# Queries and keys of two head groups transposed by VectorE and through DRAM, with 15 slots and 6 split units

## The chip, the cores and the metric

One core of a Trainium2 chip runs the whole program. The metric is the device time of one execution in microseconds (us). Engines are named as in the profile: PE is TensorE (matmul), PEld its weight load, DVE is VectorE, ACT is ScalarE, POOL is GpSimd, SP the engine that issues the DMAs.

## The reference, cut to what matters

Two layers work on x of 256 tokens and 2048 columns, in float32. Each layer mixes tokens and then channels:

```python
h = rmsnorm(x, norm_mix_pre[l])
proj = h @ w_in[l]                                # 2048 -> 5120 columns
a_q, a_k, a_v, b_glu, c_q, c_k, c_v, d_q, d_k, d_v = jnp.split(proj, split_at, axis=-1)
out_a = diff_attention(a_q, a_k, a_v, ...)        # 4 heads, two maps of 64 each, rotary
out_b = conformer_conv(b_glu, ...)                # 31 taps, layernorm, 512x512 product
out_c = gqa_axial_attention(c_q, c_k, c_v, ...)   # 4 query heads, 2 key heads of 128
out_d = neighbourhood_attention(d_q, d_k, d_v, rpb)
mixed = jnp.concatenate([out_a, out_b, out_c, out_d], axis=-1) @ w_out[l]
x = x + rmsnorm(mixed, norm_mix_post[l])
h = rmsnorm(x, norm_ffn_pre[l])
f = (silu(h @ ffn_gate[l]) * (h @ ffn_up[l])) @ ffn_down[l]   # 2048 -> 5632 -> 2048
x = x + rmsnorm(f, norm_ffn_post[l])
```

The scores of A and C are products over the head's columns, so queries and keys are needed with those columns on the partitions: transposed.

## The kernel before, in words

**Products.** Each weight is read once from DRAM in pieces of 128 rows by 1024 columns, two to a load (a `Raw`, 1 MB, three buffers). A piece is a unit. ScalarE rounds it to the short format of TensorE (`whi`, `split_hi`), VectorE computes what the rounding left (`wlo`, `split_lo`), and a product is x's rounded half times both, plus x's residual times `whi`. A step (`products`) is one unit, one of the two blocks of 128 tokens, and two PSUM banks of 512 columns: six matmuls. `NSPLIT` buffers hold split units.

**Order.** The program's order is written out by `run`, step by step. Ahead of a step's products come, in this order, the loads tied to it (`pre`), `tick`, and `splits_to`. `tick` advances every other piece of work (a generator) whose time has come by a planner's clock `at`, which adds a cost to each instruction; `wait` adds 0.2 to that clock where a step's left operand has not been issued yet. Each engine then works its own queue in that order, and semaphores do the rest. `plan` (line 261) cuts a pass over the weights into groups of units: a group's steps run for the first tokens, then for the second, and a unit's buffers come free with the second (`used`). REGULAR groups have four units. FIRST, used for the first pass of the gate/up phases and of layer 1's input phase, is 6, 5, 5. LAST is 4, 4, 3, 5.

`splits_to` (line 242) says how far the splits run ahead. It is called with `used + NSPLIT` and the unit of the step:

```python
        while self.next_split < n:
            r = self.next_split // 2
            self.loads_to(r + 1)
            self.split_hi(self.units[self.next_split])
            if self.next_split > self.next_lo:
                self.lo_next()
            self.next_split += 1
        while self.next_lo < min(needed + 1, n):
            self.lo_next()
```

**Phases of a layer.** Input (five passes, B, C, A, D and V, 160 steps), output (two passes over the mixed columns, in the order C, B, A, D in the first), gate/up (11 passes), down (two passes). Between the end of one phase and the next, `post` normalises x, adds it, and `transpose_x` (line 421) turns it: TensorE transposes four blocks of 128 into PSUM, ScalarE writes the rounded half of `xT`, VectorE the residual half.

**Heads.** When C's projection has left PSUM, `norm_c` (line 837) normalises and rotates it in `rotC`; `rope_a` (line 736) does A's in `rotA`. Then `attn_c` (line 873) and `attn_a` (line 794) call `heads_transposed` (line 762): four (for C's keys two) TensorE transposes into a PSUM bank of the pool `tp`, and a ScalarE copy into `qkC` or `qkA`, for each block of tokens. The heads follow, two at a time: `head_c` claims one of the two `sc` banks for its scores, `head_a` both; maximum on VectorE, exponentials on ScalarE, the probabilities transposed by TensorE (`probs_transposed`). D does the same with one bank (`head_d`). `out_a` (line 999) starts when V has left PSUM and all four A heads are done, and writes `mixA`; the output phase needs it at its 17th step.

**Through DRAM.** The hidden layer of the gate/up phase already goes another way: `ffn_half` (line 531) lets VectorE transpose 32x32 blocks, SP writes them to DRAM (`h_blocks`), and `turned` (line 551) reads them back so that the blocks' order is put right (`ht`), from where ScalarE and VectorE make `hT`.

**Slots.** All wider working tiles share one pool of `SLOTS` buffers of 8 KB per partition. A split unit has two buffers of 4 KB.

Of the kernel before, what the change touches and what calls it, by code (L numbers as in the profile page):

```python
# [11 lines left out]
F32 = mybir.dt.float32  # L12
F32R = mybir.dt.float32r
AF = mybir.ActivationFunctionType
# [5 lines left out]
P = 128  # L20
L = 2
S = 256
T = S // P
# [9 lines left out]
HD = 128  # L33
RPB = 15 * 31

SLOTS = 14
NRAW = 3
NSPLIT = 7
RAMP = 3
CONV_LEAD = 1.5  # L40
LATENCY = 0.4
LC_AT = 12
STATS_AT = 20
# [59 lines left out]
class Trunk:  # L103
# [214 lines left out]
    def tick(self):  # L318

        todo, self.gens = self.gens, []  # L320
        kept = []
        for entry in todo:
            g, ready = entry
            if ready <= self.at["PE"]:
                self.chain = 0.0
                try:
                    next(g)
                except StopIteration:
                    continue
                entry[1] = self.chain + LATENCY if self.chain else 0.0  # L330
            kept.append(entry)
        self.gens = kept + self.gens

# [402 lines left out]
    def rope_a(self, phase, pair, tok):  # L736
# [21 lines left out]
        if tok == T - 1:  # L758
            yield from self.until(T, "a", phase)
            yield from self.attn_a()  # L760

    def heads_transposed(self, dst, src, n):

        nc = self.nc
        for tok in range(T):
            yield from self.claim("tp")
            b = self.bank("tp", (4, P))
            for h in range(n):
                nc.tensor.transpose(b[:, h], src(tok)[:, h * P:(h + 1) * P], self.ident)
            yield  # L770
            nc.scalar.activation(dst[:, 0:n, tok * P:(tok + 1) * P], b[:, 0:n], AF.Copy)
            yield
            self.free("tp")
# [18 lines left out]
        self.free("tp")  # L792

    def attn_a(self):
        qk = self.slot([2, 4, S], F32, "qkA")
        for i in range(2):
            yield from self.heads_transposed(qk[:, i], lambda t: self.rotA[:, t, i], 4)
        self.ptA = self.slot([4, T, S], F32, "ptA")
        work = self.slot([2, 2, T, S], F32, "workA")
        for h in range(4):  # L800
            yield from self.until(h - 1, "done_a", self.l)
            self.spawn(self.head_a(h, qk, work[:, h % 2]))
            yield

    def head_a(self, h, qk, p):
        nc = self.nc
        yield from self.claim("sc", 2)
        banks = [self.bank("sc", (T, S)) for _ in range(2)]
        for t in range(T):
            for m in range(2):  # L810
                rows = slice(m * 64, (m + 1) * 64)
                nc.tensor.matmul(banks[m][:, t], qk[rows, 0, h, t * P:(t + 1) * P], qk[rows, 1, h],
                                 start=True, stop=True)
        yield
        mx, sm = self.small(4, "mx"), self.small(4, "sm")
        for m in range(2):
            nc.vector.reduce_max(mx[:, 2 * m:2 * m + 2], banks[m], axis=AX.X)
        nc.vector.tensor_scalar(mx, mx, -0.125, None, op0=ALU.mult)
        for m in range(2):
            self.exps(p[:, m], banks[m], mx[:, 2 * m:2 * m + 2], sm[:, 2 * m:2 * m + 2], 0.125)  # L820
        yield
        self.free("sc", 2)
        nc.vector.reciprocal(sm, sm)
        nc.vector.tensor_scalar(sm[:, 2:4], sm[:, 2:4], self.neg_lam[:, self.l:self.l + 1], None,
                                op0=ALU.mult)
        for t in range(T):
            nc.scalar.activation(p[:, 1, t], p[:, 1, t], AF.Copy, scale=sm[:, 2 + t:3 + t])
        yield
        for t in range(T):
            nc.vector.scalar_tensor_tensor(p[:, 0, t], p[:, 0, t], sm[:, t:t + 1], p[:, 1, t],  # L830
                                           op0=ALU.mult, op1=ALU.add)
        yield
        yield from self.probs_transposed(p[:, 0], self.ptA[:, h])
        self.mark("done_a", self.l)
# [36 lines left out]
            yield from self.attn_c()  # L871

    def attn_c(self):
        qk = self.slot([6, S], F32, "qkC")
        yield from self.heads_transposed(qk[:, 0:4], lambda t: self.rotC[:, t, 0:512], 4)
        yield from self.heads_transposed(qk[:, 4:6], lambda t: self.rotC[:, t, 512:768], 2)
        self.mixT[2] = self.slot([2, 4, S], F32R, "mixC")
        work = self.slot([2, 2, T, S], F32, "workC")
        for h in range(4):
            yield from self.until(h - 1, "mix_c", self.l)  # L880
            self.spawn(self.head_c(h, qk, work[:, h % 2]))
            yield

    def softmax(self, p, src, scale):
# [20 lines left out]
        yield  # L905
        self.free("tp")

    def head_c(self, h, qk, work):
        nc = self.nc
        yield from self.claim("sc")  # L910
        b = self.bank("sc", (T, S))
        for t in range(T):
            nc.tensor.matmul(b[:, t], qk[:, h, t * P:(t + 1) * P], qk[:, 4 + h // 2], start=True, stop=True)
        yield
        p, pt = work[:, 0], work[:, 1]
        sx = self.softmax(p, b, HD ** -0.5)
# [133 lines left out]
    def build(self):  # L1050
# [4 lines left out]
        for l in range(L):  # L1055
# [9 lines left out]
            if l == 0:  # L1065
                self.steps[n0 + 8].pre += [self.tables]
                self.steps[n0 + 44].pre += [lambda: self.spawn(self.lambdas())]
            self.steps[n0 + 108].pre += [lambda l=l: self.load_bias(l)]
            self.steps[n0 + 120].pre += [self.mask_bias]
            w = a["w_out"][l]  # L1070
            n0 = len(self.steps)
            order = [4 * "ABCD".index(g) + i for g in OUT_ORDER for i in range(4)]
# [94 lines left out]
```

## Time and profile before

| what | value |
|---|---|
| time, median of 3 runs | 2179.38 us (2179.23 to 2179.76) |
| time of the profiled execution | 2179.6 us |
| its span, first to last instruction | 2177.8 us |
| TensorE busy | 2156.9 us, 99% of the span |
| VectorE busy | 1271.1 us, 58% |
| ScalarE busy | 1093.8 us, 50% |
| mean granted TensorE clock | 0.999 |
| bytes moved by DMA | 447.52 MB, 205 GB/s over the span |

A busy share says how long an engine had an instruction in it. TensorE's matmul records overlap, so a share of 99% says that it hardly ever stood empty, and the spacing of the records, not their length, says what one costs. Nearly all instructions carry line 89, the line of the helper that records their cost, so work is found by the names of its tiles.

### The profile page before, as it was taken

How to read it: one execution, taken by the hardware profiler on the slowest of the kernel's cores; microseconds unless marked ns; L12 is line 12 of the kernel's file. 1: busy time of each engine (PE TensorE's matmuls, PEld its weight loads, DVE VectorE, ACT ScalarE, POOL GpSimd, SP SyncE). 2: the span in 40 equal slices, each digit the busy share in tenths (PEclk: the TensorE clock that was granted, in tenths of full speed). 3: DMA queues.
4: the chain of work that ended last, by engine and by line, in shares of the span. 5: the costliest groups of instructions: out<-in, count | busy, mean ns of one | idle time of the engine just before them, and what ended most of it. 6: DMA issues, size and time to landing. Idle time of an engine off the chain costs nothing.

```text
span 2177.8 us, 25210 instructions
## 1 busy us (share of the span) xinstructions
PE 2156.9 (99%) x9720; PEld 1781.5 (82%) x9720; DVE 1271.1 (58%) x1520; ACT 1093.8 (50%) x1398; POOL 28.6 (1%) x38
## 2 busy tenths in 40 slices
PE   8999999999999999999999999999999999999998
PEld 7888887888888888888878888878888888888886
DVE  5898555555555554444468975555555555554444
ACT  6656754544444444343465576554444444443432
POOL 0000000000000000000000000000000000000000
PEclk9999999999999999999999999999999999999999
DMA  7556446766676666555575563557667666765553
GB/s 277 194 177 184 170 149 221 232 213 212 223 222 213 212 223 221 214 193 194 211 237 182 191 188 136 210 187 241 213 221 223 213 213 222 223 213 213 193 218 130
DMA packets 200281, 447.52 MB, mean 205 GB/s; under 512 B 20704, under 2 KB 43744, under 8 KB 197856
## 3 DMA queue, kind: packets, MB, share of 16 engines
q1 hardware_dynamic: 200016, 445.87, 60.5%
q8 instruction: 76, 1.25, 0.2%
q14 instruction: 45, 0.37, 0.1%
q10 hardware_dynamic: 144, 0.03, 0.0%
HBM read 425.93 MB, written 19.92 MB: 205 GB/s over the span
## 4 chain that ended last, share of the span: by engine, by line
PE 97%; ACT 1%; DVE 1%; issue 0%; DMA 0%; DVEq 0%; POOLq 0%; ACTq 0%
PE acc L89 93%; PE tp L89 3%; PE sc L89 1%; ACT whi L89 0%; DVE xT L89 0%; ACT workA L89 0%; DVE x L89 0%; ACT L89 0%; DMA x<-in_x_dram 0%; ACT xT L89 0%; DVE mx L89 0%; DVE wlo L89 0%; ACT conv L89 0%; ACT qkD L89 0%; ACT junk L89 0%
## 5 line engine op out<-in xcount | busy, mean ns | idle before, releaser
L89 PE MATMUL acc<-whi,xT 128*128 128x512 f32 x4096 | 1293.3, 393 | 6.8 <-DVE xT L89 2.9
L89 PEld LDWEIGHTS acc<-whi,xT 128*128 128x128 f32 x4096 | 769.9, 188 | 171.5 <-DVE xT L89 5.5
L89 PE MATMUL acc<-wlo,xT 128*128 128x512 f32 x2048 | 799.1, 390 | 0.5 <-DVE wlo L89 0.5
L89 ACT ACTIVATE whi<-raw,gains 128x1024 fp32r<-128x1024 f32 x512 | 582.6, 1150 | 388.6 <-PE acc L89 365.8
L89 DVE SCALAR_TENSOR_TENSOR wlo<-raw,gains,whi 128x1024 fp32r<-128x1024 f32 x512 | 641.8, 1278 | 216.9 <-ACT whi L89 208.8
L89 PEld LDWEIGHTS acc<-wlo,xT 128*128 128x128 f32 x2048 | 385.3, 188 | 78.6 <-DVE wlo L89 1.0
L89 DVE TENSOR_TENSOR wlo<-raw,whi 128x1024 fp32r<-128x1024 f32 x240 | 292.5, 1223 | 260.6 <-ACT whi L89 243.9
L89 PE MATMUL acc<-whi,hT 128*128 128x512 f32 x1408 | 434.1, 389 | 0.0
L89 ACT ACTIVATE whi<-raw 128x1024 fp32r<-128x1024 f32 x240 | 253.7, 1060 | 304.3 <-PE acc L89 304.1
L89 PEld LDWEIGHTS acc<-whi,hT 128*128 128x128 f32 x1408 | 264.3, 188 | 54.9
L89 PE MATMUL acc<-wlo,hT 128*128 128x512 f32 x704 | 273.9, 389 | 0.0
L89 PEld LDWEIGHTS acc<-wlo,hT 128*128 128x128 f32 x704 | 132.1, 188 | 27.3
L89 DVE TENSOR_TENSOR hT<-ht,hT 128x1024 fp32r<-128x1024 f32 x22 | 27.0, 1225 | 142.3 <-ACT hT L89 142.3
L89 DVE SCALAR_TENSOR_TENSOR h<-acc,rstd,h 128x512 f32<-128x512 f32 x44 | 33.0, 751 | 120.9 <-ACT h L89 120.9
L89 DVE SCALAR_TENSOR_TENSOR conv<-uT,lc,conv 128x256 f32<-128x256 f32 x240 | 99.3, 480 | 0.0
L89 ACT ACTIVATE hT<-ht 128x1024 fp32r<-128x1024 f32 x22 | 23.3, 1059 | 107.5 <-DMA ht<-h_blocks 107.5
L89 ACT ACTIVATE h<-acc,rstd 128x512 f32<-128x512 f32 x44 | 30.3, 688 | 81.5 <-PE acc L89 81.2
L89 ACT ACTIVATE junk<-acc 128x512 bf16<-128x512 f32 x32 | 19.1, 595 | 55.9 <-PE acc L89 53.0
L89 PE MATMUL acc<-whi,mixC 128*128 128x512 f32 x128 | 44.7, 402 | 0.0
L89 PE MATMUL acc<-whi,mixB 128*128 128x512 f32 x128 | 42.2, 397 | 0.0
L89 DVE TENSOR_TENSOR mg<-acc,gpost 128x512 f32<-128x512 f32 x32 | 21.3, 686 | 35.8 <-PE acc L89 19.5
L89 PE MATMUL acc<-whi,mixD 128*128 128x512 f32 x128 | 41.6, 391 | 0.0
(136 smaller groups left out, 962.2 us busy)
## 6 DMA issues: line engine op xcount, KB each, us to landing
raw<-in_ffn_gate_dram SPq DMA_DIRECT2D x176, 512.0 KB, 3.9
raw<-in_ffn_up_dram SPq DMA_DIRECT2D x176, 512.0 KB, 5.1
raw<-in_ffn_down_dram SPq DMA_DIRECT2D x88, 1024.0 KB, 5.0
raw<-in_w_in_dram SPq DMA_DIRECT2D x63, 1024.0 KB, 5.1
raw<-in_w_out_dram SPq DMA_DIRECT2D x32, 1024.0 KB, 5.0
raw<-in_w_in_dram SPq DMA_DIRECT2D x34, 512.0 KB, 4.7
h_blocks<-blocks SPq DMA_DIRECT2D x44, 256.0 KB, 5.5
ht<-h_blocks SPq DMA_DIRECT2D x88, 128.0 KB, 5.3
```

The source lines that it names most:

```text
L89: return f(*args, **kw)
```

## The change

VectorE transposes queries and keys of A and C in blocks of 32x32 (`crossed`). SP writes the blocks to DRAM, one DMA per block of tokens, and reads them back with four DMAs of 32 partitions each. ScalarE copies the queries into order, for A into the buffer that later takes the probabilities, for C back into `rotC`; the keys are used where they landed, in runs of 32 columns. The planner lets 9.0 pass by its clock after each of the two transfers. The pool has one slot more and the splits one unit less. The bias loads of D and their mask are tied to later steps.

```diff
--- before.py
+++ after.py
@@ -33,11 +33,12 @@
 HD = 128
 RPB = 15 * 31
 
-SLOTS = 14
+SLOTS = 15
 NRAW = 3
-NSPLIT = 7
+NSPLIT = 6
 RAMP = 3
 CONV_LEAD = 1.5
+TRANSFER = 9.0
 LATENCY = 0.4
 LC_AT = 12
 STATS_AT = 20
@@ -324,10 +325,12 @@
             if ready <= self.at["PE"]:
                 self.chain = 0.0
                 try:
-                    next(g)
+                    transfer = next(g)
                 except StopIteration:
                     continue
                 entry[1] = self.chain + LATENCY if self.chain else 0.0
+                if transfer:
+                    entry[1] = max(entry[1], self.at["PE"] + TRANSFER)
             kept.append(entry)
         self.gens = kept + self.gens
 
@@ -759,6 +762,32 @@
             yield from self.until(T, "a", phase)
             yield from self.attn_a()
 
+    def crossed(self, srcs, n, name, dst):
+
+        w = n * P
+        hd = self.pd.tile([S, w], F32, name=self.name(name))
+        qk = self.slot([2048], F32, name)
+        for tok in range(T):
+            bt = qk[:, tok * 1024:tok * 1024 + w]
+            for h0 in range(0, n, 4):
+                m = min(4, n - h0)
+                out = bt.rearrange("p (q k n) -> p k q n", q=4, k=n)[:, h0:h0 + m]
+                src = srcs(tok, h0, m).rearrange("p (k q n) -> p k q n", k=m, q=4)
+                self.nc.vector.transpose(out, src)
+            yield
+            self.nc.sync.dma_start(hd[tok * P:(tok + 1) * P, :], bt)
+        yield True
+        qk = qk[:, 0:8 * n * 32].rearrange("p (t k n) -> p t k n", t=8, k=n)
+        for q in range(4):
+            src = hd[:, q * n * 32:(q + 1) * n * 32].rearrange("(t p) m -> p t m", p=32)
+            self.nc.sync.dma_start(qk[32 * q:32 * q + 32].rearrange("p t k n -> p t (k n)"), src)
+        yield True
+        for h, (out, m) in enumerate(dst):
+            q = qk[:, :, h * m:(h + 1) * m].rearrange("p t h n -> p h t n")
+            self.nc.scalar.activation(out.rearrange("p h (t n) -> p h t n", t=8), q, AF.Copy)
+        yield
+        return qk
+
     def heads_transposed(self, dst, src, n):
 
         nc = self.nc
@@ -792,24 +821,23 @@
         self.free("tp")
 
     def attn_a(self):
-        qk = self.slot([2, 4, S], F32, "qkA")
-        for i in range(2):
-            yield from self.heads_transposed(qk[:, i], lambda t: self.rotA[:, t, i], 4)
         self.ptA = self.slot([4, T, S], F32, "ptA")
+        q = self.ptA[:, :, 0]
+        qk = yield from self.crossed(lambda t, h, n: self.rotA[:, t, h // 4], 8, "qkA", [(q, 4)])
         work = self.slot([2, 2, T, S], F32, "workA")
         for h in range(4):
             yield from self.until(h - 1, "done_a", self.l)
-            self.spawn(self.head_a(h, qk, work[:, h % 2]))
-            yield
-
-    def head_a(self, h, qk, p):
+            self.spawn(self.head_a(h, q[:, h], qk[:, :, 4 + h], work[:, h % 2]))
+            yield
+
+    def head_a(self, h, q, k, p):
         nc = self.nc
         yield from self.claim("sc", 2)
         banks = [self.bank("sc", (T, S)) for _ in range(2)]
         for t in range(T):
             for m in range(2):
                 rows = slice(m * 64, (m + 1) * 64)
-                nc.tensor.matmul(banks[m][:, t], qk[rows, 0, h, t * P:(t + 1) * P], qk[rows, 1, h],
+                nc.tensor.matmul(banks[m][:, t], q[rows, t * P:(t + 1) * P], k[rows],
                                  start=True, stop=True)
         yield
         mx, sm = self.small(4, "mx"), self.small(4, "sm")
@@ -871,14 +899,13 @@
             yield from self.attn_c()
 
     def attn_c(self):
-        qk = self.slot([6, S], F32, "qkC")
-        yield from self.heads_transposed(qk[:, 0:4], lambda t: self.rotC[:, t, 0:512], 4)
-        yield from self.heads_transposed(qk[:, 4:6], lambda t: self.rotC[:, t, 512:768], 2)
+        q = [self.rotC[:, t, 0:512].rearrange("p (h s) -> p h s", h=2) for t in range(T)]
+        qk = yield from self.crossed(lambda t, h, n: self.rotC[:, t, h * P:(h + n) * P], 6, "qkC", [(x, 2) for x in q])
         self.mixT[2] = self.slot([2, 4, S], F32R, "mixC")
         work = self.slot([2, 2, T, S], F32, "workC")
         for h in range(4):
             yield from self.until(h - 1, "mix_c", self.l)
-            self.spawn(self.head_c(h, qk, work[:, h % 2]))
+            self.spawn(self.head_c(h, q[h // 2][:, h % 2], qk[:, :, 4 + h // 2], work[:, h % 2]))
             yield
 
     def softmax(self, p, src, scale):
@@ -905,12 +932,12 @@
         yield
         self.free("tp")
 
-    def head_c(self, h, qk, work):
+    def head_c(self, h, q, k, work):
         nc = self.nc
         yield from self.claim("sc")
         b = self.bank("sc", (T, S))
         for t in range(T):
-            nc.tensor.matmul(b[:, t], qk[:, h, t * P:(t + 1) * P], qk[:, 4 + h // 2], start=True, stop=True)
+            nc.tensor.matmul(b[:, t], q[:, t * P:(t + 1) * P], k, start=True, stop=True)
         yield
         p, pt = work[:, 0], work[:, 1]
         sx = self.softmax(p, b, HD ** -0.5)
@@ -1065,8 +1092,8 @@
             if l == 0:
                 self.steps[n0 + 8].pre += [self.tables]
                 self.steps[n0 + 44].pre += [lambda: self.spawn(self.lambdas())]
-            self.steps[n0 + 108].pre += [lambda l=l: self.load_bias(l)]
-            self.steps[n0 + 120].pre += [self.mask_bias]
+            self.steps[n0 + 120].pre += [lambda l=l: self.load_bias(l)]
+            self.steps[n0 + 130].pre += [self.mask_bias]
             w = a["w_out"][l]
             n0 = len(self.steps)
             order = [4 * "ABCD".index(g) + i for g in OUT_ORDER for i in range(4)]
```

## Rows read from the trace of the kernel before

**Rows 1.** The page: busy time of each engine; the chain that ended last, by engine.
```profile
PE 2156.9 (99%) x9720; PEld 1781.5 (82%) x9720; DVE 1271.1 (58%) x1520; ACT 1093.8 (50%) x1398; POOL 28.6 (1%) x38
...
PE 97%; ACT 1%; DVE 1%; issue 0%; DMA 0%; DVEq 0%; POOLq 0%; ACTq 0%
```

**Rows 2.** TensorE's waits: who waited for whom, us in total, times, longest.
```profile
PE acc L89 <- DVE wlo L89: 0.5, 1, 0.5
```

**Rows 3.** The chain in order of time: start us, us, what; the longest piece of layer 0.
```profile
384.33 701.14 PE acc L89 x3093
```

**Rows 4.** Timeline of TensorE around a group of two and one of four transposes.
```profile
144.65 0.38 PE L89 MATMUL tp<-ident,rotC 128*128 128x128 f32 x2
...
145.10 0.40 PE L89 MATMUL acc<-wlo,xT 128*128 128x512 f32 x1
...
177.57 0.60 PE L89 MATMUL tp<-ident,rotA 128*128 128x128 f32 x4
...
178.24 0.39 PE L89 MATMUL acc<-wlo,xT 128*128 128x512 f32 x1
```

**Rows 5.** Groups by form: busy us, mean ns of one, idle us before.
```profile
L89 ACT ACTIVATE whi<-raw 128x1024 fp32r<-128x1024 f32 x240 | 253.7, 1060 | 304.3 <-PE acc L89 304.1
...
L89 DVE STREAM_TRANSPOSE blocks<-h 128x512 f32<-128x512 f32 x44 | 31.0, 705 | 0.0
...
L89 ACT ACTIVATE hT<-ht 128x1024 fp32r<-128x1024 f32 x22 | 23.3, 1059 | 107.5 <-DMA ht<-h_blocks 107.5
...
L89 PE MATMUL sc<-qkA 64*128 64x256 f32 x64 | 9.1, 402 | 0.0
...
L89 PE MATMUL tp<-ident,rotA 128*128 128x128 f32 x32 | 4.8, 272 | 0.0
```

**Rows 6.** DMA issues: operation, count, KB each, median us from issue to landing.
```profile
h_blocks<-blocks SPq DMA_DIRECT2D x44, 256.0 KB, 5.5
ht<-h_blocks SPq DMA_DIRECT2D x88, 128.0 KB, 5.3
...
x<-x_spill SPq DMA_DIRECT2D x6, 1024.0 KB, 8.7
```

**Rows 7.** Timeline of TensorE at the start of layer 0's gate/up phase.
```profile
372.78 0.60 PE L89 MATMUL tp<-ident,x 128*128 128x128 f32 x4
...
373.45 0.40 PE L89 MATMUL acc<-wlo,xT 128*128 128x512 f32 x1
...
374.61 1.03 PE L89 MATMUL tp<-ident,x 128*128 128x128 f32 x8
376.38 0.50 PE L89 MATMUL acc<-whi,xT 128*128 128x512 f32 x1 [0.74 <-ACT xT L89]
```

**Rows 8.** Timeline of VectorE in the same stretch.
```profile
370.04 1.27 DVE L89 SCALAR_TENSOR_TENSOR wlo<-raw,gains,whi 128x1024 fp32r<-128x1024 f32 x1
...
374.05 0.69 DVE L89 TENSOR_TENSOR xT<-tp,xT 128x512 fp32r<-128x512 f32 x1 [0.81 <-ACT xT L89]
```

**Rows 9.** Timeline of TensorE in layer 0: C begins, A ends, A's output products begin.
```profile
135.26 0.60 PE L89 MATMUL tp<-ident,rotC 128*128 128x128 f32 x4
...
149.00 1.02 PE L89 MATMUL sc<-qkC 128*128 128x256 f32 x4
...
245.32 0.74 PE L89 MATMUL tp<-ident,workA 128*128 128x128 f32 x4 [0.19 <-DVE workA L89]
...
265.64 1.95 PE L89 MATMUL sc<-vAD,ptA 128*128 128x128 f32 x16
```

**Rows 10.** Timelines of VectorE and TensorE: mixA's last write and first use, both layers.
```profile
292.87 0.69 DVE L89 TENSOR_TENSOR mixA<-tp,mixA 128x512 fp32r<-128x512 f32 x1 [2.13 <-ACT mixA L89]
...
298.10 0.39 PE L89 MATMUL acc<-whi,mixA 128*128 128x512 f32 x1
...
1376.01 0.69 DVE L89 TENSOR_TENSOR mixA<-tp,mixA 128x512 fp32r<-128x512 f32 x1
...
1379.29 0.39 PE L89 MATMUL acc<-whi,mixA 128*128 128x512 f32 x1
```

## The prediction

> **What bounds the kernel now.** I read the page first, engine shares and the chain that ended last [rows 1]: TensorE is busy 99% of the span and holds 97% of the chain. Then TensorE's own waits [rows 2]: on the residual half of a split weight (`wlo`) it waited once, 0.5 us in all, so today no split is late. Then the chain in order of time [rows 3]: 3093 products of 512 columns follow one another in 701.14 us, 0.227 us each. A step is six of them, 1.37 us. So the time changes in two ways only: work leaves or joins TensorE's queue, or TensorE begins to wait. Anything under 0.2% (4.4 us) a measurement of this kernel cannot tell from no change.
>
> **What leaves TensorE.** Per layer, 16 transposes for A (four groups of four) and 12 for C (two groups of four, two of two): 56 in two layers. Their price is read from the queue around them. From the start of a group of four to the second product after it is 0.67 us (177.57 to 178.24), less one product 0.23: 0.44. For a group of two 0.45 less 0.23: 0.22 [rows 4]. So 12 x 0.44 + 4 x 0.22 = **6.2 us off**. The record of one transpose is 272 ns long [rows 5], but records overlap; 0.11 us each is what the queue loses. The Trainium skill, "TensorE: Matmul & The Clock Gate", Part 4: PE-mode transpose, gives about 275 ns for one in a kernel's context; the trace agrees on the record's length (272), not on its price here, and by 0.275 the 56 would be worth 15.4 us instead of 6.2.
>
> **What joins the other engines, at no cost while TensorE leads.** VectorE gets per layer four 512-wide transposes for A, two of 512 and two of 256 for C: 8 at most at 705 ns [rows 5], 5.6 us, and VectorE is 58% busy [rows 1]. ScalarE loses eight PSUM copies per layer and gets one copy of 1024 elements for A, two of 512 for C, from data cut in runs of 32; `hT`'s copy, cut the same way, takes 1059 ns for 1024, a plain one 1060 [rows 5]. So a little less work than before. SP gets 12 more DMAs per layer (two writes and four reads for each of A and C). A write waits on SP for its transposes, and weight loads stand behind it; that is short, because the order issues it a step later. The write of 256 KB takes 5.5 us, a read of 128 KB 5.3; here they are twice that or less (512 and 256 KB for A). Even 1024 KB from DRAM takes 8.7 [rows 6]. The order allows 9.0 by its own clock, in which a step costs 1.29 against 1.37 traced: about 9.6 us. So ScalarE's copies, and the weight splits queued behind them, should not wait. From above: each of the four read-backs late by 2 us, most of it inside the margin of the splits; I take 0.
>
> The score products now read the keys in runs of 32 columns at a stride. No row shows TensorE doing that. From below nothing; from above the price doubles, for A 9.1 us of records [rows 5], and about as much again for C. ScalarE reads the same runs without surcharge [rows 5], so I take 0; the upper end gets a chance of 0.02 and stays outside the range. The bias loads and the mask, moved 12 and 10 steps later, still precede D's scores; cost 0.
>
> **Six split units instead of seven.** In steady groups of four a split is issued five steps before its use instead of six, 6.9 us instead of 8.2, for 1.06 + 1.27 us of work [rows 5, 8]. No stall. But the first group of a phase has six units (FIRST: the gate/up phase of both layers, the input phase of layer 1; three places). `splits_to` issues a residual only with the *next* unit's rounded half, or when its step needs it. With seven buffers unit 6 may be split during unit 0's step, and that issues unit 5's residual. With six buffers unit 6 must wait for a buffer, so unit 5's residual is issued right ahead of its own products, after the tick of that step. That tick holds the transposes of x's third block: behind them stands, on VectorE, the residual of that block.
>
> Layer 0's gate/up start shows the price. Now VectorE finishes unit 5's residual at 371.31 (370.04 + 1.27), and TensorE reads it at 373.45. After: transposes of x at 372.78, ScalarE's rounding, VectorE's xT 374.05 to 374.74 [rows 7, 8] (that pair begins when the transposes end, so it does not come earlier), then the residual, 1.27 more, about 375.95. TensorE reads it at 376.0 instead of 373.45: **2.55 us**. Does it come back? The next eight transposes (374.61) and the product that waits for them (376.38) [rows 7] lie behind unit 5's products in TensorE's queue, so they move with it. The pattern repeats in all three places: **+7.6 us**. Bounds: 0, if the order puts the tick elsewhere, and 4 each (12), if the second group's splits, one step later too, also come late.
>
> **C and A come later.** C's first transposes are at 135.26 and its first scores at 149.00, 13.7 us [rows 9]. After: two transfers of 9.6 and about four steps of 1.4, 25 us. So C's heads move by some eight or nine steps, and A's heads, which queue for the same two score banks, with them. A step here takes 1.75 us with its insertions (149.00 to 245.32 is 55 steps), so A's last probabilities (245.32) come near 261 in layer 0; with their copy the output products, now at 265.64 [rows 9] for lack of V, would start about 5.4 us later, in layer 1 about 3.2 by the same count (two steps). The margins now: mixA's last write ends at 293.56 for a use at 298.10 (4.5 us); in layer 1 1376.70 for 1379.29 (2.6) [rows 10]. Short by 0.9 and 0.6: **+1.5 us**. Bounds 0 and 12 (below).
>
> **The sum.** -6.2 + 7.6 + 1.5 = +2.9. The profiled execution took 2179.6 us, its span 2177.8; the median is 2179.4, 0.2 lower, so the same sum stands against it: **2182.3 us**. Its own range, with no A shortfall at one end and twice it plus 1.5 at the other, is 2180 to 2186.
>
> **Rivals.**
> 1. *A loses the score banks (slower).* A head needs both banks at once, a D head one. If D's first two heads reach the queue before A's fourth, A's output starts two to four steps later still, and no margin is left: 3.5 to 7 us more than my sum if in layer 0 alone, 2186 to 2189, and 13.4 more, 2195.7, if in both layers. It decides from a delay of 4.5 us on, layer 0's margin. For it: D's transposes need not move, and A's last pair moves onto D's start. Against it: A's fourth head is queued first if it is released on time. Chance 0.28, of which 0.08 for both layers.
> 2. *No stop at the phase starts (faster).* If unit 5's residual is issued earlier than I read, only -6.2 + 1.5 is left: 2174.7, with no shortfall 2173.2. Against it stands the code of `splits_to`. Chance 0.11.
> 3. *A transpose costs its whole record.* 56 x 0.272 = 15.2 off: -15.2 + 7.6 + 1.5 gives 2173.3. Against it the spacing [rows 4]. Chance 0.04.
> 4. *Transposes belong on TensorE.* VectorE transposes only 32x32 blocks, and the detour through DRAM (5.5 and 5.3 us [rows 6]) makes the route dearer wherever it is waited for: if the scores waited unhidden, ScalarE's queue and the splits with it, some 3 us for each of four read-backs, 2194. The Trainium skill, "VectorE: DVE Perf Modes", Rules for kernel authors, says so in general: for 128x128 take TensorE if PSUM will do as the destination. Against it here: no scores are waited for by TensorE's main products. Chance 0.05.
>
> My sum has 0.50. **How the numbers follow.** Over 2183.8 (slower by 0.2%) lie rivals 1 and 4, dear score reads (together 0.35) and the upper part of my own case (0.05): slower 0.40. Under 2175.0 lie rivals 2 and 3, nearly all: faster 0.12. Same: 0.48. The range 2174.5 to 2191 leaves out rival 3 and half of rival 2 below (0.09), rival 1 in both layers and part of the rest above (0.11); it takes in the bounds of the phase starts (0 and 12).
>
> **What would show it.** Right: three TensorE waits on `wlo` of about 2.5 us each, near 373 in layer 0 and at the same point of the two other phase starts, beside 0.5 us in all now [rows 2]; the groups of transposes from rotA and rotC gone from TensorE, their 56 records with them; no wait of ScalarE on the read-back; strided score records as long as now. A's shortfall shows as a TensorE wait on mixA at the first A product of the output phase, under 2 us; in rival 1 it is over 5, and D's scores stand ahead of A's fourth. Wrong: no wait on `wlo` (rival 2), longer score records, or new waits on `whi` in the attention stretch, which would mean that six buffers are too few there as well.

## The result, and the profile after

| | before | after |
|---|---|---|
| median | 2179.31 us (2179.08 to 2179.76, 4 runs) | 2206.34 us (2201.94 to 2207.65, 4 runs) |
| profiled execution, its span | 2179.6 us, 2177.8 us | 2206.11 us, 2204.1 us |

The ratio is 1.012 [1.0108, 1.0132]: 27 us slower, and outside the forecast range of 2174.5 to 2191.

The page after: busy time of each engine, and the chain that ended last by engine, against [rows 1].

```profile
PE 2160.6 (98%) x9664; PEld 1780.3 (81%) x9664; DVE 1284.7 (58%) x1536; ACT 1096.7 (50%) x1388; POOL 28.6 (1%) x38
...
PE 86%; DVE 6%; ACT 5%; issue 1%; DMA 1%; SPq 1%; POOL 0%; DVEq 0%; POOLq 0%; ACTq 0%
```

56 matmuls have left TensorE (9720 to 9664), as foretold, yet it is busy 3.7 us longer, and its share of the chain fell from 97% to 86%: for much of the attention stretch other engines now set the pace. That fewer instructions are busy for longer hints at a slower clock. TensorE's waits after (who waited for whom, us in total, times, longest), against [rows 2]:

```profile
PE acc L90 <- DVE wlo L90: 9.1, 5, 2.4
...
PE tp L90 <- DVE mixB L90: 4.2, 3, 2.0
PE acc L90 <- ACT vAD L90: 3.6, 1, 3.6
```

The first line is the forecast stop at the phase starts. The others are in no part of the forecast. To see where the 27 us came from I laid the two traces side by side by step: the start of a step is the start of its first product of 512 columns, and the table gives the difference after minus before. (Layer 0's first B product, for instance, starts at 284.91 before and 295.24 after: 10.3.)

| the first product of | before, us | after | difference |
|---|---|---|---|
| layer 0: output phase, C | 264.27 | 259.03 | -5.2 |
| B in that phase | 284.91 | 295.24 | +10.3 |
| gate/up phase | 364.77 | 375.68 | +10.9 |
| the same, second group's first step | 386.94 | 401.96 | +15.0 |
| layer 1: input phase | 1089.17 | 1104.22 | +15.0 |
| the same, 28 steps on | 1133.12 | 1152.51 | +19.4 |
| output phase, C | 1346.69 | 1355.96 | +9.3 |
| B in that phase | 1365.57 | 1388.01 | +22.4 |
| gate/up phase | 1445.05 | 1467.94 | +22.9 |
| the same, second group's first step | 1467.19 | 1494.20 | +27.0 |
| the last step of the kernel | 2168.27 | 2195.30 | +27.0 |

Read as sums: the input phases gain 5.2 and 10.1; the output phases lose 16.1 and 13.6, nearly all of it ahead of the first B product; the three phase starts lose 4.1, 4.4 and 4.1; 12.6 together. So the input and output phases without the starts, called the attention stretches below, lose 14.3 in all. Everywhere else, some 1500 us, the two agree to 0.2 us a stretch.

**B's place.** Before, B's mix was written long ahead of its use; I had looked at A's margins only [rows 10]. Two lines of the kernel before, from the timelines of VectorE and TensorE:

```profile
271.63 0.47 DVE L89 SCALAR_TENSOR_TENSOR mixB<-tp,lc,mixB 128x256 fp32r<-128x256 f32 x1
...
284.91 0.39 PE L89 MATMUL acc<-whi,mixB 128*128 128x512 f32 x1
```

From the end of the write (272.1) to the use that is 12.8 us of margin; in layer 1 it was 28.2. In the kernel after it is 0.5 in both. The timeline of TensorE after, in the same place (start us, us, what, and the idle time before it with its releaser):

```profile
275.72 0.62 PE L90 MATMUL acc<-whi,mixC 128*128 128x512 f32 x2
...
277.04 1.89 PE L90 MATMUL tp<-conv,pw 128*128 128x256 f32 x8
...
281.74 1.99 PE L90 MATMUL tp<-conv,pw 128*128 128x256 f32 x8 [1.95 <-DVE mixB L90]
...
285.98 1.99 PE L90 MATMUL tp<-conv,pw 128*128 128x256 f32 x8 [1.81 <-ACT ptA L90]
...
290.03 1.89 PE L90 MATMUL tp<-conv,pw 128*128 128x256 f32 x8
...
294.83 0.66 PE L90 MATMUL tp<-ident,oA 128*128 128x128 f32 x4 [2.04 <-DVE mixB L90]
295.24 0.48 PE L90 MATMUL acc<-whi,mixB 128*128 128x512 f32 x1
```

Between the last C product and the first B product 19 us pass in which no product of the main stream runs: all four blocks of B's last product (`conv` times `pw`, 2 us each) stand there in the written order, each with its copies behind it, because `run` calls `wait` until step 168's left operand has been issued, and little else was left to put there. Each wait is only 2 us and names an engine that was not late by itself; the loss is the whole stretch.

**Why B is late.** B's convolution is 124 taps a layer on VectorE, and `fill` and `conv` hand them out only while VectorE's planner clock is less than `CONV_LEAD` ahead of TensorE's. VectorE's timeline after, layer 0:

```profile
198.70 2.29 DVE L90 TENSOR_TENSOR bias<-bias,tables 128x2048 f32<-128x2048 f32 x1 [0.20 <-DMA qkA<-qkA]
...
210.52 2.07 DVE L90 SCALAR_TENSOR_TENSOR conv<-uT,lc,conv 128x256 f32<-128x256 f32 x5
...
218.31 2.06 DVE L90 SCALAR_TENSOR_TENSOR conv<-uT,lc,conv 128x256 f32<-128x256 f32 x5
...
220.63 0.48 DVE L90 SCALAR_TENSOR_TENSOR conv<-uT,lc,conv 128x256 f32<-128x256 f32 x1
```

The last eleven taps of the layer stand behind the mask and end at 221.1; before they ended at 196.7, after a mask at 189.0. TensorE's first transposes of `conv` start at 233.8, before at 202.4. The late taps are only the first part of it. Against the run with loads and mask back (below) the last tap ends in step 141 instead of 136 in layer 0, and in step 134 in both kernels in layer 1; the first transposes of `conv` come 9 and 5 steps later, the first products with `pw` 13 and 12 (steps 167 and 165 instead of 154 and 153). So B falls further behind after its taps, where its pieces take turns with those of A, C and D. What holds them there no run tried.

**The phase start.** TensorE and VectorE after, layer 0's gate/up start, against [rows 7, 8]:

```profile
384.05 0.48 PE L90 MATMUL acc<-whi,xT 128*128 128x512 f32 x1
386.89 0.78 PE L90 MATMUL acc<-wlo,xT 128*128 128x512 f32 x1 [2.37 <-DVE wlo L90]
387.47 0.63 PE L90 MATMUL acc<-whi,xT 128*128 128x512 f32 x1
```

```profile
384.96 0.69 DVE L90 TENSOR_TENSOR xT<-tp,xT 128x512 fp32r<-128x512 f32 x1 [0.81 <-ACT xT L90]
385.57 1.27 DVE L90 SCALAR_TENSOR_TENSOR wlo<-raw,gains,whi 128x1024 fp32r<-128x1024 f32 x1
```

That is the step as the prediction told it: the residual of unit 5 directly behind that of x's third block, done at 386.84, read at 386.89. What it left out shows in the records that follow: 0.63 us where a product had 0.40. The view by stretches gives the clock (columns: stretch, its length, busy time and count by engine, PEclk = granted clock, share of the DMA engines, GB/s):

```profile
380.00:386.50 6.50, 4.53 (x22) 3.48 (x21) 5.66 (x10) 2.92 (x9) 0.56 (x1) 1.00 0.99 325
386.80:390.30 3.50, 3.40 (x11) 2.82 (x12) 0.04 (x1) 0.03 (x1) 0.00 (x0) 0.52 0.74 248
391.00:398.00 7.00, 6.04 (x27) 4.69 (x28) 4.26 (x8) 3.62 (x5) 0.55 (x1) 1.00 0.03 10
```

After the stop of 2.37 us the granted clock is 0.52, the lower of its two levels (1.2 of 2.4 GHz) but for an edge, and then 1.00 again.

### The profile page after: what moved, and what is told of

It is laid out like the page before. It is cut to its first block, busy times and chain, and to the rows that moved or that the text cites. A ratio compares the mean times of both kernels' runs of the same rounds, so it can differ in the third digit from the quotient of the medians.

```text
span 2204.1 us, 25158 instructions
## 1 busy us (share of the span) xinstructions
PE 2160.6 (98%) x9664; PEld 1780.3 (81%) x9664; DVE 1284.7 (58%) x1536; ACT 1096.7 (50%) x1388; POOL 28.6 (1%) x38
## 4 chain that ended last, share of the span: by engine, by line
PE 86%; DVE 6%; ACT 5%; issue 1%; DMA 1%; SPq 1%; POOL 0%; DVEq 0%; POOLq 0%; ACTq 0%
PE acc L90 83%; DVE wlo L90 2%; PE tp L90 2%; ACT whi L90 1%; DVE conv L90 1%; ACT workA L90 1%; PE sc L90 1%; DVE mx L90 1%; ACT workD L90 1%; SPq L625 0%; DVE xT L90 0%; ACT L90 0%; ACT junk L90 0%; DMA lc<-in_heads_dram 0%; ACT workC L90 0%
## 5 line engine op out<-in xcount | busy, mean ns | idle before, releaser
L90 PEld LDWEIGHTS acc<-wlo,xT 128*128 128x128 f32 x2048 | 385.6, 188 | 89.1 <-DVE wlo L90 10.9
L90 DVE TENSOR_TENSOR xT<-tp,xT 128x512 fp32r<-128x512 f32 x32 | 22.0, 688 | 41.5 <-ACT xT L90 41.5
L90 DVE TENSOR_TENSOR mg<-acc,gpost 128x512 f32<-128x512 f32 x32 | 21.3, 686 | 34.9 <-PE acc L90 19.5
```

Source lines behind the costliest of these rows:

```text
L90: return f(*args, **kw)
```

## The experiments

All ratios are against the kernel before on the same chip. "B's stretch" is the time from step 164 to 168 in layer 0 and from 936 to 940 in layer 1: 9.7 and 8.3 us before, 26.1 and 19.4 after.

**The six units alone.** The kernel before with one number changed.

```diff
-NSPLIT = 7
+NSPLIT = 6
```

> The kernel before with six split units, nothing else. If the residual of the sixth unit is what stops TensorE at the three phase starts, three waits on wlo of about 2.5 us come, and with the half clock that the changed kernel's trace shows after two of them (3.4 us at 0.5, so 1.7 us each) the time is 2187 to 2192 us. Rival: six units cost nothing by themselves, and the waits in the changed kernel belong to its other work: 2179 to 2181.

Measured 2192.1 us, 1.0054 [1.0037, 1.0071]. TensorE's wait:

```profile
PE acc L89 <- DVE wlo L89: 9.3, 5, 2.4
```

The three starts lose 4.1, 4.6 and 4.1 us, 12.8 by steps, as in the kernel after, and nothing else moves: B's stretches are 9.7 and 8.3. Three stops of 2.4 us make 7.2; the second group's residual at layer 1's input start is late too (2.0), and after two of the stops the clock is granted at half, 1.7 us each. The stretch behind the first stop:

```profile
375.60:379.00 3.40, 3.35 (x11) 2.77 (x12) 0.00 (x0) 0.00 (x0) 0.00 (x0) 0.51 0.79 264
```

**The residuals two units ahead.** The kernel after; in the three places `splits_to` is told to have the residuals ready two units further ahead.

```diff
-            self.splits_to(min(used + NSPLIT, i + RAMP), s.unit.index)
+            ahead = 2 if s.pair == 0 and s.phase in (("gu", 0), ("in", 1), ("gu", 1)) else 0
+            self.splits_to(min(used + NSPLIT, i + RAMP), s.unit.index + ahead)
```

> The changed kernel, with residuals issued up to two units ahead of the step in the first pass of the three phases whose first group has six units. If the phase starts cost what the traces say (4.2, 2.6 and 4.2 us, and 1.8 behind the second), the three waits on wlo go and 9 to 13 us come back: 2193 to 2197. Rival: VectorE only does the same work in another order and x's transposed blocks come late instead: 2202 to 2206, with waits on xT in place of wlo.

Measured 2195.01 us, 1.0072 [1.0057, 1.0087]: 11 us less than after. The wait on `wlo` is 0.5 us again, as in [rows 2], and the starts lose nothing (under 0.05 us each). B's stretch in layer 0 is as long as after (26.7). So six buffers are enough at the starts once the residual is issued earlier, and this gain leaves B's loss as it was.

**The bias loads back.** After each read-back ScalarE had waited. ScalarE's waits after, and SP's timeline in layer 0:

```profile
ACT ptA L90 <- DMA qkA<-qkA: 12.4, 2, 8.0
...
ACT rotC L90 <- DMA qkC<-qkC: 6.7, 1, 6.7
```

```profile
182.76 10.60 SPq L625 DMA_DIRECT2D bias<-in_na_rpb_rev_dram  x16
193.40 2.08 SPq L783 DMA_DIRECT2D qkA<-qkA  x4
```

The sixteen bias loads hold SP's queue for 10.6 us right ahead of A's read-back. The edit puts them where they stood before; the mask stays late.

```diff
-            self.steps[n0 + 120].pre += [lambda l=l: self.load_bias(l)]
+            self.steps[n0 + 108].pre += [lambda l=l: self.load_bias(l)]
```

> The changed kernel with D's bias loads at step 108 again, as before the change (the mask stays at 130); every engine's order but SP's is the same. Theory A: the loss in the output phases comes from B's late place in the written order, so the time stays within 3 us of 2206, although ScalarE no longer waits 4.4 and 8.0 us for A's read-back. Rival: the 10.6 us of bias loads ahead of A's read-back in SP's queue hold ScalarE and with it everything behind: 8 to 16 us come back, 2190 to 2198.

Measured 2201.94 us, 1.0104 [1.0089, 1.0119]: 4.4 us less than after, a little more than the 3 that the expectation allowed. ScalarE's wait for A's read-back falls to 2.7 us, but B's stretches stay at 27.0 and 19.4. By the steps of the profiled executions, 4.9 us apart, 3.2 of the gain lie at the phase starts, which this edit does not touch (9.4 lost there instead of 12.6), and 1.6 in the attention stretches (about 3, if one allows for the half-clock stretch more that fell into them). So the queue costs little here; it is not the cause.

**The mask back as well.**

```diff
-            self.steps[n0 + 120].pre += [lambda l=l: self.load_bias(l)]
-            self.steps[n0 + 130].pre += [self.mask_bias]
+            self.steps[n0 + 108].pre += [lambda l=l: self.load_bias(l)]
+            self.steps[n0 + 120].pre += [self.mask_bias]
```

> The changed kernel with the bias loads at step 108 and the mask at 120, both as before the change. The mask is 2.3 us of VectorE in the stretch where the taps of B's convolution are given out. Theory A (B's place in the order): the taps end earlier, B's mix is issued ahead of its first use in layer 0, and 8 to 16 us come back, 2190 to 2198, more than in the run with the loads alone by at least 5 us. Rival (SP's queue): the same as the run with the loads alone, within 2 us.

Measured 2192.84 us, 1.0061 [1.0046, 1.0076]: 9 us less than with the loads alone. B's stretches are 8.0 and 9.4 us, and B's mix ends 10 us ahead of its use in both layers. The taps now run on behind a mask at 183.81, the last two groups being

```profile
200.70 4.42 DVE L90 SCALAR_TENSOR_TENSOR conv<-uT,lc,conv 128x256 f32<-128x256 f32 x11
...
208.42 1.66 DVE L90 SCALAR_TENSOR_TENSOR conv<-uT,lc,conv 128x256 f32<-128x256 f32 x4
```

done at 210.1 instead of 221.1; the transposes of `conv` begin at 216.2 instead of 233.8. By steps, the attention stretches lose 3.9 us against the kernel before, where they lost 14.3 in the kernel after and 12.7 with the loads alone put back. What is late next is A's mix in layer 1, 8.9 us between steps 944 and 948, on TensorE:

```profile
1387.99 1.16 PE L90 MATMUL tp<-ident,oA 128*128 128x128 f32 x4 [3.55 <-DVE oA L90]
```

**Both mended**: loads and mask back, residuals early (the two edits above together).

> The changed kernel with the bias loads and the mask at 108 and 120 again, and residuals up to two units ahead in the three first passes: the edits of the second and the fourth run together. If phase starts and B's place are two separate losses, the gains add: 2206.3 less 13.5 less 11.3 (and a half-clock stretch more or less) is 2179 to 2183, with A's mix still late in layer 1 (8.9 us at its first use). Rival: one covers the other, as both only bring forward work of VectorE: 2186 or more.

Measured 2183.17 us, 1.0016 [1.0007, 1.0025]. The gains add: 13.5 (mask and loads) and 11.3 (residuals) from 2206.34 give 2181.5, within 2 us of it. With the residuals early in both kernels, loads and mask are worth 11.8 (2195.01 to 2183.17). What keeps it above the kernel before is A's late mix in layer 1, 8.9 us.

**D before A.** The same, with A, the last to be ready, put last.

```diff
-IN_ORDER, OUT_ORDER = "BCADV", "CBAD"
+IN_ORDER, OUT_ORDER = "BCADV", "CBDA"
```

> As the run before, and the output phase takes D's mix ahead of A's (C, B, D, A), since A is now the last to be ready. If what is left is A's late mix in layer 1, 8 to 11 us come back less what D's own lateness costs (2 to 4): 2172 to 2177, under both kernels. Rival: D is as late as A, because both wait for the same score banks: 2179 or more.

Measured 2177.01 us, 0.9988 [0.9979, 0.9997], a gain of 2.5 us. TensorE's waits sum to 15.1 us against 12.1 before, the span is 2.6 us shorter (2175.2): without the 3.0 us of new waits the change would have taken off 5.6 us. That estimate is as near as these runs come to the worth of the 56 transposes: it is a difference of two executions that are also unlike in order, slots and split units.

**The order alone**, on the kernel before.

> The kernel before with the output order C, B, D, A in place of C, B, A, D and nothing else. The fastest kernel so far (2177.0 us) has this order and the change's transposes. Theory: the order helps there because A is late with the transposes by VectorE; in the kernel before A's margin was 4.5 and 2.6 us and D's 7.2 and 14.3 us, so putting D ahead gains nothing and takes D's margin away: 2179 to 2186 us. Rival: the order gains by itself, 2174 to 2178 us, and the fastest kernel owes its gain to the order and not to the transposes.

Measured 2179.99 us, 1.0002 [0.9992, 1.0012]. No change: the order by itself gains nothing. By steps the fastest kernel gains 2.4 us in layer 0's attention stretch, loses 0.4 in layer 1's and nothing at the phase starts. That the gain comes from the transposes fits this, but the fifteenth slot was in no run by itself.

**The move of loads and mask alone**, on the kernel before.

```diff
-            self.steps[n0 + 108].pre += [lambda l=l: self.load_bias(l)]
-            self.steps[n0 + 120].pre += [self.mask_bias]
+            self.steps[n0 + 120].pre += [lambda l=l: self.load_bias(l)]
+            self.steps[n0 + 130].pre += [self.mask_bias]
```

> The kernel before with one part of the change alone: the sixteen bias loads at step 120 instead of 108 and the mask at step 130 instead of 120; seven split buffers, fourteen slots, all transposes by TensorE. My theory after the fourth run: the late mask hurts because it meets VectorE's transposes and the later heads; alone it meets VectorE where group B's taps still have room, so B's mix stays ahead and the loss is below 5 us: 2177 to 2184 us, steps 164 to 168 within 1 us of the kernel before. Rival: the late mask by itself pushes B's taps into the output phase; then steps 164 to 168 and 936 to 940 lose 10 to 17 us each, and the time is 2195 us or more.

Measured 2179.06 us, 0.9996 [0.9987, 1.0005]. B's stretch in layer 0 is 11.1 us (1.4 more than before, where the expectation allowed 1), in layer 1 6.5, and B's margin in layer 0 is 10.3. VectorE's timeline in layer 0:

```profile
191.60 2.05 DVE L89 SCALAR_TENSOR_TENSOR conv<-uT,lc,conv 128x256 f32<-128x256 f32 x5
...
210.61 2.29 DVE L89 TENSOR_TENSOR bias<-bias,tables 128x2048 f32<-128x2048 f32 x1
```

Here the last taps are done before the mask comes. That alone does not tell the kernels apart: 7 taps of layer 0 stand behind the mask in the kernel before and 31 with loads and mask back, and B is in time in both. What the runs do show is that the move costs nothing by itself and 13.5 us with the rest of the change (4.4 and 9.1 in the two runs above): it is the two together.

**A alone.** The kernel after, C's transposes by TensorE as before. The edit puts the old `attn_c` and `head_c` back; these are its first lines:

```diff
-        qk = yield from self.crossed(lambda t, h, n: self.rotC[:, t, h * P:(h + n) * P], 6, "qkC", [(x, 2) for x in q])
+        qk = self.slot([6, S], F32, "qkC")
+        yield from self.heads_transposed(qk[:, 0:4], lambda t: self.rotC[:, t, 0:512], 4)
+        yield from self.heads_transposed(qk[:, 4:6], lambda t: self.rotC[:, t, 512:768], 2)
```

> The changed kernel, with C's queries and keys transposed by TensorE again; A crosses through DRAM, six units, the late bias loads and mask stay. If C's crossing is what moves B (its transposes on VectorE and its heads' later start meet the taps), B is in time: 2179.4 less 3.5 for A's 32 transposes, plus 12.5 for the six units, plus 0 to 6 for A: 2188 to 2195. Rival: A's crossing or the late mask alone is enough: 2200 or more.

Measured 2207.25 us, 1.0126 [1.0111, 1.0142]: my theory missed. B is in time (margins 21.8 and 15.7 us), so C's detour is needed for B's loss; but a new loss stands in the input phase, 14.4 us between steps 128 and 144. SP, ScalarE and TensorE, three timelines:

```profile
188.79 10.99 SPq L625 DMA_DIRECT2D bias<-in_na_rpb_rev_dram  x16
199.83 2.22 SPq L783 DMA_DIRECT2D qkA<-qkA  x4
```

```profile
210.38 1.06 ACT L90 ACTIVATE ptA<-qkA 128x1024 f32<-128x1024 f32 x1 [13.60 <-DMA qkA<-qkA]
```

```profile
211.49 2.15 PE L90 MATMUL sc<-qkA,ptA 64*128 64x256 f32 x8 [10.04 <-ACT ptA L90]
213.57 0.80 PE L90 MATMUL acc<-whi,xT 128*128 128x512 f32 x1
```

The same queue that cost little in the full change stops TensorE for 10 us here: its first scores of A start at 211.49, right behind ScalarE's copy of the queries. The granted clock is at half in that stretch:

```profile
204.00:217.00 13.00, 5.51 (x18) 4.15 (x19) 3.77 (x5) 4.83 (x7) 0.00 (x0) 0.50 1.00 297
```

**A alone, seven units.** The same with 14 slots, seven split buffers, the loads at step 112, the mask at 124, and a shorter allowance for a transfer (`TRANSFER = 5.0`).

> A crosses alone; seven units and 14 slots as before the change, the bias loads at 112 and the mask at 124, 5.0 allowed for a transfer. Nothing is left but the 32 transposes of A that TensorE no longer does, 32 x 0.11 = 3.5 us, if no mix comes late: 2175 to 2177. Rival: the read-back, allowed less time, holds ScalarE and A's mix comes late: 2180 or more.

Measured 2198.59 us, 1.0086 [1.0072, 1.01]: missed too. There is no stop at the phase starts, which again fits their cause, and B and A are in time, but TensorE waits in the input phase:

```profile
PE tp L90 <- ACT workC L90: 9.8, 3, 6.3
PE sc L90 <- ACT ptA L90: 5.0, 1, 5.0
```

With 5.0 allowed, the scores are written before the read-back can have landed; ScalarE waits for it 7.1 us in layer 0 and 6.7 in layer 1, where C's probabilities stand behind it in ScalarE's queue and TensorE behind those:

```profile
1289.76 1.06 ACT L90 ACTIVATE ptA<-qkA 128x1024 f32<-128x1024 f32 x1 [6.69 <-DMA qkA<-qkA]
1290.72 0.89 ACT L90 ACTIVATE workC<-workC,sm 128x256 f32<-128x256 f32 x2
```

```profile
1291.26 1.11 PE L90 MATMUL tp<-ident,workC 128*128 128x128 f32 x4 [6.31 <-ACT workC L90]
```

The allowance, the loads' place and the units were changed together here, so their shares stay open.

**A alone, loads and mask back.** The kernel of "A alone" with the loads at 108 and the mask at 120.

> The changed kernel with group C's transposes by TensorE again (as in the run of A alone) and the bias loads and the mask back at steps 108 and 120. In the run of A alone ScalarE waited 13.6 us for A's read-back, which stood in SP's queue behind the sixteen bias loads (188.8 to 199.8 us), and TensorE waited 10.0 us for the scores that follow. Theory (the queue): with the loads gone from there the read-back starts some 9 us sooner, TensorE's wait of 10.0 us falls below 3 us in layer 0, and the time falls by 8 to 16 us, to 2191 to 2199 us, the stops at the phase starts (12 us) still in it. Rival (A's two transfers one after the other are what TensorE waits for, loads or not): the wait stays at 5 us or more, and the time above 2200 us.

Measured 2187.77 us, 1.0034 [1.0021, 1.0047]: 19.5 us less, more than the theory's 8 to 16. ScalarE's waits for the read-back fall from 24.3 us to 5.1, the longest from 13.6 to 3.2, and TensorE waits for the scores no more. The loads go out at 162.36 and the read-back at 188.87 instead of 199.83. The theory's sum had counted the stop of layer 0 (10.0) and the phase starts; it left out layer 1's, which was 7.2 us, and the clock, which is at half for 27 us of the work in "A alone" and stays full in the work here. The mask was moved back together with the loads; that the loads do it is read from the three timelines above. TensorE's waits on `ptA` in "A alone", both layers:

```profile
PE sc L90 <- ACT ptA L90: 17.2, 2, 10.0
```

**The fastest without C.** The kernel with D before A, C's transposes by TensorE again.

> The fastest kernel so far (2177.0 us: residuals early, loads and mask back at steps 108 and 120, D before A) with group C's transposes by TensorE again, so that only A's 32 of the 56 transposes a pass leave TensorE. Theory: the run of A alone with the loads back took 2187.8 us with the stops at the phase starts in it; without them some 11 to 12 us less, and with D ahead A's late mix of 1 to 3 us goes too: 2173 to 2177 us, no more than the kernel with both groups. Rival: C's transposes by VectorE are worth their own share (24 x 0.11 us by layer, 5 us in both layers), and without them the time is 2179 us or more.

Measured 2176.65 us, 0.9987 [0.9978, 0.9996]: not to be told from the kernel with both groups (0.9988). C's 24 transposes are worth nothing on balance: what they take off TensorE, their detour gives back in waits (15.1 us in all with C's, 13.1 without). The rival's price was a slip of mine: the 24 are those of both layers, 2.6 us at 0.11 each and not 5.

## Why the prediction was wrong, point by point

- **"The bias loads and the mask, moved 12 and 10 steps later, still precede D's scores; cost 0."** This step failed, and it is most of the miss. I asked who reads the bias and not what the mask is put in front of: on VectorE it now stands 10 us later than before (198.70 for 189.01), ahead of B's last taps. Loads and mask back gave 13.5 us by the medians and 10.5 by the steps of the attention stretches, the mask 9.1 and 8.9 of it. The same move costs nothing without the new transposes, and the late mask leaves B in time without C's detour ("A alone"). That the two together make B late is shown; the way from the mask to B's late product is followed only in part ("Why B is late").
- **Margins of one group only.** The prediction read A's margin [rows 10] and took B's for safe unread. B had 12.8 us in layer 0 and 28.2 in layer 1, and they were gone. And the loss is larger than the lateness: where B is short, the written order puts a whole chain of B's work before step 168, 19 us without a main product. The prediction's rival for a late group had the right shape (a slower output phase) and the wrong group: in the kernel after A loses nothing, since TensorE has waited for B already. Why `conv`'s transposes come 12.7 us after the last tap instead of 5.7 (196.7 to 202.4 before) I did not try; in the trace transposes of C, D and A stand ahead of them.
- **"A's fourth head is queued first if it is released on time."** It was not, and one of rival 1's two signs is there: D's scores stand ahead of A's fourth. In the kernel before, all four of A's heads (the last at 228.3) have their scores ahead of D's first (247.3). After, the first two of D's, at 235.67 and 238.35, stand ahead of A's third (245.19) and fourth (254.22):

```profile
235.67 1.02 PE L90 MATMUL sc<-qkD 128*128 128x256 f32 x4
...
245.19 1.13 PE L90 MATMUL sc<-qkA,ptA 64*128 64x256 f32 x8
```

C's first scores came 14 steps later and A's last 16 and 12, where eight or nine had been taken. B's lateness hides the price in this kernel.

- **A's mix, +1.5.** Mis-sized, and hidden in the kernel after. With the mask back A's mix is late in layer 1 alone, by 8.9 us where 0.6 was taken: A's fourth scores stand 17 steps later there than before. Of the 8.9, 3.55 are one wait on `oA`, and the clock is at half behind it (products of 0.63 us instead of 0.39). Without the phase starts the forecast's terms give 2182.3 - 7.6 = 2174.7; the kernel with both losses mended takes 2183.2, 8.5 more, and with A last it takes 2177.0.
- **Six units, +7.6.** The mechanism, the three places and the 2.55 us (2.37 to 2.44) were right. The term was mis-sized: 12.6 us in the kernel after, 12.8 alone. The second group is late at one start (1.8; this was the upper bound's reason), and the clock, to which I gave nothing, costs 1.5 to 1.7 us after two of the stops.
- **"ScalarE's copies ... should not wait. I take 0."** Wrong: ScalarE waited 12.4 and 6.7 us. Each transfer lands in time by itself (below), but the loads stand ahead of the read-back in SP's queue, whose place I had not counted for the moved step. By steps that cost 1.6 to 3 us in this kernel, in "A alone" 17.2 in two stops, and the clock. So the rival that the detour is dearer wherever it is waited for was given 0.05 and is what "A alone" did.
- **-6.2 for the transposes.** Right as far as the runs can tell: 5.6 by the estimate from the fastest kernel, and 1.5 us a layer for C's group by the steps 64 to 96, where only C's transposes lie, against 2 x 0.44 + 2 x 0.22 = 1.3 foretold. Taking a transpose by its record (rival 3) would have been 15.2. The input phases' 5.2 and 10.1 look larger since work of B and A left them for the output phases (in each layer B's products with `pw` and eight of A's sixteen transposes of probabilities).
- **The strided keys, 0.** Right. Groups by form after, against 402 in [rows 5] for A, and 378 before for C:

```profile
L90 PE MATMUL sc<-qkA,ptA 64*128 64x256 f32 x64 | 11.3, 407 | 0.8 <-ACT workC L90 0.4 <-ACT workA L90 0.2 <-ACT ptA L90 0.2
L90 PE MATMUL sc<-qkC,rotC 128*128 128x256 f32 x32 | 8.2, 378 | 0.0
```

- **VectorE's and ScalarE's own work, and the transfers' durations.** Right: 686 and 708 ns a transpose where 705 was taken, 1058 ns for the copy where 1060 was, and landings where "twice that or less" was said. Groups and DMA issues after:

```profile
L90 DVE STREAM_TRANSPOSE qkC<-rotC 128x512 f32<-128x512 f32 x4 | 2.8, 708 | 0.0
```

```profile
qkA<-qkA SPq DMA_DIRECT2D x4, 512.0 KB, 6.6
qkA<-qkA SPq DMA_DIRECT2D x8, 256.0 KB, 6.5
```

So the prices of single operations were right, and what failed were covers that had been named and not measured. Of the 24 us by which the time was missed, 5.0 are the phase starts' clock and second group (12.6 less 7.6). The other 19 lie in the attention stretches, which lost 14.3 us by the steps where the terms gave a gain of 4.7 (-6.2 + 1.5). Putting the loads and the mask back takes 10.5 of the 14.3 away; most of what is left after that is A's place in layer 1.

## What to carry to other kernels

When work is moved later, list for every engine that it uses, SP's queue included, what now stands behind it there, and read that work's margin before its consumer, not the moved work's own. Read the margins of all groups that share a stage, the comfortable ones too: a kernel whose order is written out by a planner passes from no cost to a whole chain ahead of the main stream when one is used up. And try a part of a change both alone and beside the rest: here the late mask was free alone, and the detour for A was free once loads and mask were in their old place, the residuals early and D ahead of A.

## What the runs showed of the hardware that was not expected

**Short stops cost clock as well.** A stop of TensorE by 2.37 us was followed by products at half the granted clock (0.52 from 386.80 to 390.30), at two of three like places; after the 10.04 us stop in "A alone" 13 us passed at 0.50. In the kernel before no stop inside the work is that long (its longest waits are 4.6 us at the very start, then 1.7 at most) and the granted clock is 0.999 over the span. The same stop is not always followed by it: in the profiled run of "A alone, loads and mask back" the three starts lost 2.6, 3.3 and 2.6 us without a half clock. And ahead of C's products in layer 0 TensorE waited for `vAD` 3.60 us in the kernel after and 3.59 with the loads back; the clock behind it was full in the first and half in the second:

```profile
269.10:272.50 3.40, 3.40 (x16) 2.62 (x17) 1.87 (x3) 3.38 (x6) 0.00 (x0) 1.00 0.01 5
266.50:269.60 3.10, 3.08 (x7) 2.48 (x8) 1.58 (x2) 2.39 (x5) 0.00 (x0) 0.50 0.01 5
```

So such a stop at a phase start has a price of 2.6 or of 4.1 us, and which of the two is not settled by its length here. The Trainium skill, "TensorE: Matmul & The Clock Gate", Why this matters for your kernels, advises against longer idle gaps between bursts of products, because the clock falls back to half after them. The traces agree on the fall, show it after a stop of 2.37 us too, and show that it does not come each time.

**Small loads are dear where they are issued.** Sixteen loads of 64 KB kept SP's queue 10.60 us in the kernel after and 11.20 in "A alone, loads and mask back" (layer 0), about 0.7 each, though the median one is landed 4.3 us after its issue. The Trainium skill, "DMA: Bandwidth & Descriptors", Rules for kernel authors, says that spreading DMAs over engines brings no bandwidth and only saves issue time; issue time is what A's read-back waited for here. No run tried another engine's queue for them.
